# Out-projection of a two-layer encoder: early products placed by hand in the last head, and the first MLP weight splits queued behind the last pair's split

## The chip, the cores and the metric

The kernel runs on one core of one Trainium2 chip. The core has a matrix engine (TensorE, PE in the profile; its weight loads are the row PEld), a vector engine (VectorE, DVE), an activation engine (ScalarE, ACT), a general engine (GpSimd, POOL) and a queue that issues DMAs (SyncE, SP). Each engine executes its own queue in order and waits on semaphores for the others. The metric is the device time of one execution in microseconds (us); less is better.

## The reference, cut to what matters

Two layers over a sequence of 512 tokens with 1024 features, in float32. Each layer does, with shifts, scales and gates from a conditioning vector:

```
h  = rms_norm(x, g) * (1 + sc1) + sh1
q_d, k_d, v_d, cq, ckv, k_rope = split(h @ w_in)
o_dil = dilated_attention(q_d, k_d, v_d)        # 8 heads of 64
o_mla = latent_attention(cq, ckv, k_rope)       # 8 heads of 64
x  = x + gt1 * (concat[o_dil, o_mla] @ w_out)   # the out-projection
h  = rms_norm(x, g) * (1 + sc2) + sh2
x  = x + gt2 * (square(relu(h @ W1)) @ W2)      # the MLP, 4096 wide
```

The change is about the line of the out-projection and what stands next to it: the last heads of the latent attention before it, the norm and the MLP behind it.

## The kernel before

**Precision by splitting.** Every large float32 operand x is split into hi = round(x) in the PE's faster format and lo = x - hi. A product is then three matmuls into the same PSUM bank: hi by hi, lo by hi and hi by lo (`mm3`, L237 to L240). `load_split` (L229) loads a weight tile into a `raw` buffer by DMA (L232), makes hi on ACT (L233) and lo on POOL (L234).

**Layout.** x is held transposed, as eight tiles of 128 features by 512 tokens (`xT`, j = 0 to 7). A product with the token axis cut in two (`HALF`) is 256 columns wide.

**Attention.** Eight pairs of heads run one after the other (stages st = 0 to 7; pairs 0 to 3 dilated, 4 to 7 latent). `head` (L327) does, for each of four query blocks qb: scores into a PSUM bank `sc` (two buffers), the row maximum on DVE (L346), the exponential on ACT (L347), a reciprocal (L348), the scaling on ACT, DVE or POOL (L351 to L355), four transposes on PE into a bank `tr` (L358, two buffers), and the split of the transposed block (hi on ACT, L361; lo on DVE, L362) into `pt` buffers. Behind the four blocks come sixteen value products (L368), and the two halves of their result are added into the pair's `o` (ACT L370, DVE L371). Once both heads of a pair are done, `o` is split into `ot`: hi on ACT (L651), lo on POOL (L652). These splits, `OT[0]` to `OT[7]`, are what the out-projection multiplies: its input features are 8 groups of 128, one for each pair.

**Out-projection.** `out_dil(j)` multiplies the four dilated pairs, full width, in the stages of the latent heads, and adds into x (`add_x`, L659). `out_lat(j, p, hf, ks, ...)` multiplies the latent pairs ks for one half of the tokens: for k = 0, 1, 2 that needs only the first three latent pairs, for k = 3 the last pair. For the first half the program does k = 0 to 2 for all eight j behind the heads: j = 4 to 7 are added into x at once, j = 0 to 3 are held in the four `mm` banks; then k = 3 for all j. Then `norm` of the first half, all of the second half (8 x 12 matmuls), `norm` of the second half, and the MLP, whose first product takes the first half. The norm squares x tile by tile on ACT (L255, L258), sums on DVE (L259), sums over partitions with a matmul by ones (L284), and makes h in eight chunks.

**The MLP's weights.** `w1_tile(i)` is a `load_split` into the `pt` buffers (i = 0, 1; the last head's own buffers before), the `qk` buffers (i = 2, 3) or the `wh`, `wl` buffers.

**What sets the order.** The program is traced as Python runs it. `heads` is a generator that yields after each query block and after the values, ten times for a pair; `weave` calls the events of the stage whose due time (in yields, table TUNE) is past. The traced order is only a priority: a planner walks through the program with its own model of each instruction's time, and puts on every engine's queue, at each moment, the earliest traced instruction that it takes to be ready and whose buffers are free. So instructions that are ready early move ahead of earlier traced ones that wait. `tc.keep_in_program_order(ins)` ties one instruction behind the one traced just before it on the same engine; it ties nothing else. On the chip the queues are then served strictly in the planned order.

## Time and profile before

| | |
|---|---|
| runs | 1353.67 us median of 3 (1353.58 to 1356.93) |
| profiled execution | 1351.23 us, of which the trace spans 1349.5 us |
| mean granted clock of PE | 0.973 |
| PE busy | 1271.8 us |
| DMA | 167.62 MB, 124 GB/s on average |

A row of the timeline gives start, duration, engine, line of the program, operation and tiles (out<-in), and in brackets how long the engine was idle before it and who ended that. A row of the table by windows gives, for a stretch of the span, its length, and for each engine the busy time and the number of instructions; PEclk is the clock that PE was granted, 1.00 being full speed. Matmuls overlap in PE, so that the distance between two starts and not the duration of one says what a matmul costs in a row of them. The heads of the last pair (stage 7) run from 311.59 to 336.32 us in layer 0 and from 951.00 to 973.41 in layer 1, counted from the start of L370 for the head before to the first product of the last pair.

### The profile page before, as it was taken

To read this page: it belongs to the slowest core of one execution; us is meant where nothing else is said; L and a number is where in the kernel's file an instruction comes from. 1 tells how busy PE (TensorE), PEld (TensorE's weight loads), DVE (VectorE), ACT (ScalarE), POOL (GpSimd) and SP (SyncE) were. 2 spreads that over 40 slices of the span, in tenths; PEclk is the share of its full clock that TensorE was granted. 3 is DMA by queue.
4 is the path that set the end of the run, shared out by engine and by line. 5 is a ranking of instruction groups with operands and counts; after the bars stand their busy time and mean duration, and the time that the engine had idled before them with its cause. 6 is when DMAs were issued, how large, how long until landed. Compare 5 with 4: busy or idle time off the path is not lost.

```text
span 1349.5 us, 19637 instructions
## 1 busy us (share of the span) xinstructions
PE 1271.8 (94%) x7114; PEld 1116.2 (83%) x7114; DVE 761.6 (56%) x1644; ACT 680.4 (50%) x1421; POOL 653.0 (48%) x504
## 2 busy tenths in 40 slices
PE   4889989898999999999999999899799999999999
PEld 2778867777998888888899999798699888888888
DVE  6777787875763561834576678987573122121123
ACT  5567898776542332322247677887653232232321
POOL 5636786674445444444438333545443444444441
PEclk6979989999999999999999999999999999999999
DMA  9335543341244572754534243211111322233221
GB/s 343 113 102 173 182 155 103 105 134 62 71 164 165 185 266 94 266 172 157 167 122 129 79 136 123 85 48 63 60 51 54 103 94 94 94 99 104 94 94 63
DMA packets 57248, 167.62 MB, mean 124 GB/s; under 512 B 8640, under 2 KB 10816, under 8 KB 57152
## 3 DMA queue, kind: packets, MB, share of 16 engines
q1 hardware_dynamic: 57152, 166.38, 37.5%
q8 instruction: 56, 0.92, 0.3%
q14 instruction: 40, 0.33, 0.1%
HBM read 155.87 MB, written 10.49 MB: 123 GB/s over the span
## 4 chain that ended last, share of the span: by engine, by line
PE 66%; POOL 2%; DVE 2%; ACT 2%; issue 2%; DMA 1%; POOLq 0%; DVEq 0%; ACTq 0%
PE mm L240 20%; PE mm L238 20%; PE mm L239 20%; PE tr L368 2%; PE tr L358 1%; POOL wl L234 1%; PE sc L238 1%; PE sc L239 1%; PE sc L240 1%; POOL pt L234 1%; PE sc L482 0%; PE mm L469 0%; DVE pt L362 0%; PE sc L483 0%; PE mm L626 0%
## 5 line engine op out<-in xcount | busy, mean ns | idle before, releaser
L234 POOL TENSOR_TENSOR wl<-raw,wh 128x1024 fp32r<-128x1024 f32 (+3 forms) x174 | 395.7, 2276 | 440.1 <-ACT wh L233 436.4
L233 ACT ACTIVATE wh<-raw 128x1024 fp32r<-128x1024 f32 (+3 forms) x174 | 174.6, 1004 | 263.9 <-PE mm L240 211.7
L659 DVE SCALAR_TENSOR_TENSOR x<-mm,mod,x 128x512 f32<-128x512 f32 (+1 forms) x152 | 92.4, 620 | 255.7 <-PE mm L240 255.2
L238 PE MATMUL mm<-h,wh 128*128 128x512 f32 (+1 forms) x544 | 198.5, 365 | 0.2
L239 PE MATMUL mm<-h,wl 128*128 128x512 f32 (+1 forms) x544 | 198.1, 364 | 0.0
L240 PE MATMUL mm<-h,wh 128*128 128x512 f32 (+1 forms) x544 | 197.9, 364 | 0.0
L238 PE MATMUL mm<-ot,wh 128*128 128x512 f32 (+1 forms) x416 | 147.9, 357 | 7.3 <-ACT ot L651 5.2
L843 ACT ACTIVATE P<-mm 128x512 f32<-128x512 f32 (+1 forms) x80 | 41.1, 513 | 214.3 <-PE mm L240 208.2
L239 PE MATMUL mm<-ot,wl 128*128 128x512 f32 (+1 forms) x416 | 146.7, 354 | 0.0
L240 PE MATMUL mm<-ot,wh 128*128 128x512 f32 (+1 forms) x416 | 144.2, 354 | 2.2 <-POOL ot L652 2.2
L844 DVE SCALAR_TENSOR_TENSOR mm<-mm,P 128x512 f32<-128x512 f32 (+1 forms) x80 | 46.9, 589 | 132.1 <-ACT P L843 132.1
L238 PEld LDWEIGHTS mm<-h,wh 128*128 128x128 f32 x544 | 102.6, 189 | 16.8 <-DVE qk L846 0.6
L239 PEld LDWEIGHTS mm<-h,wl 128*128 128x128 f32 x544 | 102.7, 189 | 16.1
L240 PEld LDWEIGHTS mm<-h,wh 128*128 128x128 f32 x544 | 102.6, 189 | 16.2
L238 PE MATMUL mm<-qk,wh 128*128 128x512 f32 (+1 forms) x288 | 105.3, 366 | 1.0 <-DVE x L659 1.0
L239 PE MATMUL mm<-qk,wl 128*128 128x512 f32 (+1 forms) x288 | 105.3, 365 | 0.0
L240 PE MATMUL mm<-qk,wh 128*128 128x512 f32 (+1 forms) x288 | 105.2, 365 | 0.0
L170 DVE SCALAR_TENSOR_TENSOR pt<-pt,cb 128x1024 f32<-128x1024 f32 x56 | 100.6, 1828 | 0.0
L355 POOL TENSOR_SCALAR P<-P,hs 128x512 f32<-128x512 f32 x64 | 48.4, 756 | 106.0 <-DVE hs L348 85.2
L362 DVE TENSOR_TENSOR pt<-tr,pt 128x512 fp32r<-128x512 f32 x128 | 86.6, 683 | 19.1 <-ACT pt L361 18.5
L238 PEld LDWEIGHTS mm<-ot,wh 128*128 128x128 f32 x416 | 80.1, 193 | 19.2 <-ACT ot L651 5.7
L238 PE MATMUL mm<-wh,h 128*128 128x384 f32 x240 | 81.0, 352 | 11.8 <-ACT h L742 9.8
(290 smaller groups left out, 2980.2 us busy)
## 6 DMA issues: line engine op xcount, KB each, us to landing
raw<-in_w_dram SPq DMA_DIRECT2D x64, 512.0 KB, 3.4
pt<-in_wmod_dram SPq DMA_DIRECT2D x56, 512.0 KB, 4.8
raw<-in_w2a_dram SPq DMA_DIRECT2D x48, 512.0 KB, 3.5
raw<-in_wmod_dram SPq DMA_DIRECT2D x24, 512.0 KB, 3.6
raw<-in_win_dram SPq DMA_DIRECT2D x30, 384.0 KB, 3.1
bias<-b SPq DMA_DIRECT2D x32, 256.0 KB, 2.3
raw<-in_wout_dram SPq DMA_DIRECT2D x16, 512.0 KB, 3.7
raw<-in_w2b_dram SPq DMA_DIRECT2D x16, 512.0 KB, 3.4
```

The costliest lines, as they stand in the source:

```text
L170: r = V.scalar_tensor_tensor(w, w, 1.0, cb, op0=OP.mult, op1=OP.mult, accum_out=out)
L233: A.activation(hi, raw, AF.Copy)
L234: G.tensor_tensor(lo, raw, f(hi), op=OP.subtract)
L238: T.matmul(out, sh, mh, start=first, stop=False)
L239: T.matmul(out, sl, mh, start=False, stop=False)
L240: T.matmul(out, sh, ml, start=False, stop=last)
L355: G.tensor_scalar(P, P, r_, 0.0, op0=OP.mult, op1=OP.add)
L362: V.tensor_tensor(lo, tr, f(hi), op=OP.subtract)
L368: T.matmul(po[:, HALF[qh]], vals(hd, kc), pt[qh][w][:, kc], start=(kc == 0 and w == 0), stop=(kc == 3 and w == 1))
L659: V.scalar_tensor_tensor(xT[j][:, hf], p, gt[:, j:j + 1], xT[j][:, hf], op0=OP.mult, op1=OP.add)
L843: A.activation(r, p, AF.Relu)
L844: V.scalar_tensor_tensor(p, p, 0.0, r, op0=OP.max, op1=OP.mult)
```

## The change

It has two parts. The first concerns the out-projection's products for the first half of the tokens with k = 0, 1, 2. They are now traced inside the last pair's heads, by a function `early(j)`: j = 0, 1, 2 as events with due times 5.5, 6.5 and 7.5 of stage 7, that is in the second head of the pair behind query blocks 0, 1 and 2; j = 3 behind the last block's scores, j = 4 behind its transposes, j = 5 and 6 behind the values (by calls of a `hook` in `head`); j = 7 behind the heads. The first matmul of each but j = 7 is tied to the PE instruction traced just before it. j = 0 to 3 are now added at once and j = 4 to 7 held, the other way round than before, and k = 3 begins with the held ones. The out-projection's weights of the latent half are due earlier (0.5 to 5 instead of 3.5 to 10.04).

The second part traces the MLP's weight tiles 0 to 3 right behind the heads instead of at the MLP, and ties the ACT half and the POOL half of tile 0 to the instructions traced just before them on ACT and POOL, which are the last pair's split (L651 and L652).

```diff
-    OL0=(3.5, 3.5), OL1=(10.04, 10.04), MV0=(1.5,), MV1=(3.75,), MV2=(5.37,), MV3=(8,), MV4=(0.62,),
+    OL0=(0.5, 0.5), OL1=(5, 5), OE=(5.5, 5.5), MV0=(1.5,), MV1=(3.75,), MV2=(5.37,), MV3=(8,), MV4=(0.62,),
...
-    def load_split(src, n, raw="raw", tags=("wh", "wl")):
+    def load_split(src, n, raw="raw", tags=("wh", "wl"), keep=False):
         SY.dma_start(raw, src)
-        A.activation(hi, raw, AF.Copy)
-        G.tensor_tensor(lo, raw, f(hi), op=OP.subtract)
+        ra = A.activation(hi, raw, AF.Copy)
+        rg = G.tensor_tensor(lo, raw, f(hi), op=OP.subtract)
+        if keep:
+            tc.keep_in_program_order(ra)
+            tc.keep_in_program_order(rg)
...
-    def mm3(out, sh, sl, mh, ml, first, last):
-        T.matmul(out, sh, mh, start=first, stop=False)
+    def mm3(out, sh, sl, mh, ml, first, last, pin=False):
+        r = T.matmul(out, sh, mh, start=first, stop=False)
+        if pin:
+            tc.keep_in_program_order(r)
...
+            if qb == 3:
+                hook("score")
...
+            if qb == 3:
+                hook("turned")
...
+        hook("values")
...
+                hook = (lambda at: [early(j) for j in EARLY[at]]) if st == 7 and hd else (lambda at: None)
+                yield from head(l, 2 * pr + hd, hd, w["score"], bias, w["vals"], o, hook)
...
+        EARLY = dict(score=(3,), turned=(4,), values=(5, 6))
+        held = {}
+
+        def early(j, pin=True):
+            p = ps("mm")[:, :256]
+            out_lat(j, p, HALF[0], (0, 1, 2), True, j < 4, pin)
+            if j < 4:
+                add_x(j, HALF[0], p, gt1)
+            else:
+                held[j] = p
...
+                ev += [(tn("OE") + j, lambda j=j: early(j)) for j in range(3)]
...
+        ws1 = [w1_tile(i, i == 0) for i in range(4)]
+        hf = HALF[0]
+        early(7, False)
         for j in (4, 5, 6, 7, 0, 1, 2, 3):
-            p = ps("mm")[:, :256]
-            out_lat(j, p, hf, (0, 1, 2), True, j >= 4)
-            if j >= 4:
-                add_x(j, hf, p, gt1)
-            else:
-                held[j] = p
-        for j in range(8):
-            p = held[j] if j < 4 else ps("mm")[:, :256]
-            out_lat(j, p, hf, (3,), j >= 4, True)
+            p = held[j] if j >= 4 else ps("mm")[:, :256]
+            out_lat(j, p, hf, (3,), j < 4, True)
             add_x(j, hf, p, gt1)
...
-            ws = [w1_tile(i) for i in range(8)] if grp[0] == 0 else []
+            ws = ws1 + [w1_tile(i) for i in range(4, 8)] if grp[0] == 0 else []
```

More of the change, by code (lines that the diff above doesn't have):

```diff
@@ L325, in distances, with head @@
         return dist, g
-    def head(l, h, hd, score, bias, vals, o):
+    def head(l, h, hd, score, bias, vals, o, hook=lambda at: None):
         pt = [(t4("pt", [128, 4, 256]), t4("pt", [128, 4, 256])) for _ in range(2)]
@@ L648, in heads @@
             for hd in range(2):
-                yield from head(l, 2 * pr + hd, hd, w["score"], bias, w["vals"], o)
+                hook = (lambda at: [early(j) for j in EARLY[at]]) if st == 7 and hd else (lambda at: None)
+                yield from head(l, 2 * pr + hd, hd, w["score"], bias, w["vals"], o, hook)
             ot = t4("h" if st in (2, 3) else "ot", [128, 2, S])
@@ L665, in out_load, with out_lat @@
             wo[half, jj] = (hi.rearrange("p (j k m) -> p j k m", j=2, k=4), lo.rearrange("p (j k m) -> p j k m", j=2, k=4))
+        EARLY = dict(score=(3,), turned=(4,), values=(5, 6))
+        held = {}
+        def out_lat(j, p, hf, ks, first, last, pin=False):
+            wh, wl = wo[1, j // 2]
+            for k in ks:
+                mm3(p, wh[:, j % 2, k], wl[:, j % 2, k], OT[4 + k][:, 0, hf], OT[4 + k][:, 1, hf],
+                    first and k == ks[0], last and k == ks[-1], pin and k == ks[0])
+        def early(j, pin=True):
[5 more added lines that the diff above has]
+                held[j] = p
         def out_dil(j):
@@ L805, in trunk, with w1_tile @@
         h2h, h2l = new_h()
[L807 to L825 removed]
+        def w1_tile(i, pin=False):
+            tags = ("wh", "wl") if i >= 4 else ("pt", "pt") if i < 2 else ("qk", "qk")
+            return tuple(t.rearrange("p (k m) -> p k m", k=8) for t in load_split(a["w1"][l, i], 1024, tags=tags, keep=pin))
+        ws1 = [w1_tile(i, i == 0) for i in range(4)]
+        hf = HALF[0]
+        early(7, False)
+        for j in (4, 5, 6, 7, 0, 1, 2, 3):
+            p = held[j] if j >= 4 else ps("mm")[:, :256]
+            out_lat(j, p, hf, (3,), j < 4, True)
             add_x(j, hf, p, gt1)
@@ L846, in mlp1_post @@
             V.tensor_tensor(r2[:, 1, hf], p, f(r2[:, 0, hf]), op=OP.subtract)
-        def w1_tile(i):
-            tags = ("wh", "wl") if i >= 4 else ("pt", "pt") if i < 2 else ("qk", "qk")
-            return tuple(t.rearrange("p (k m) -> p k m", k=8) for t in load_split(a["w1"][l, i], 1024, tags=tags))
         R2 = {}
```

6 lines of the change are left out of this document (removed).

## The prediction

> **What bounds the kernel now.** I read the page first, then the busy time of each engine by stage, then the timelines of PE, POOL and ACT around the end of attention in both layers.
>
> ```profile
> span 1349.5 us, 19637 instructions
> ...
> PE 1271.8 (94%) x7114; PEld 1116.2 (83%) x7114; DVE 761.6 (56%) x1644; ACT 680.4 (50%) x1421; POOL 653.0 (48%) x504
> ```
>
> PE is busy for 94% of the span, so only two things can pay: time in which PE is idle, and time in which its clock is low. Both must be looked for in the stage that the change touches. I cut layer 1 at the starts of L370, which each head executes once behind its last value product; the last two borders are the first product of the last pair and the first MLP product.
>
> ```profile
> core 0: us, PE busy (x) PEld busy (x) DVE busy (x) ACT busy (x) POOL busy (x), PEclk, DMA share, GB/s
> ...
> 934.05:942.72 8.67, 8.67 (x62) 7.67 (x61) 6.14 (x13) 7.29 (x17) 4.90 (x4) 1.00 0.18 60
> 942.72:951.00 8.28, 7.33 (x46) 5.63 (x44) 6.15 (x13) 6.80 (x16) 1.33 (x3) 1.00 0.01 2
> 951.00:963.69 12.69, 11.43 (x84) 10.27 (x83) 7.79 (x17) 8.35 (x17) 5.31 (x5) 1.00 0.04 13
> 963.69:973.41 9.72, 5.52 (x43) 4.66 (x40) 4.21 (x7) 8.28 (x13) 4.55 (x2) 1.00 0.25 94
> 973.41:992.74 19.33, 17.50 (x123) 16.92 (x124) 11.80 (x30) 9.08 (x19) 10.06 (x6) 0.82 0.30 93
> ```
>
> Rows one and two are the next-to-last pair's heads, three and four the last pair's, five the rest of the out-projection. The last head keeps PE busy for only 5.52 of 9.72 us, and in the last row the clock is 0.82. Layer 0 has the same shape:
>
> ```profile
> 291.00:303.05 12.05, 9.22 (x54) 7.97 (x53) 9.23 (x16) 9.48 (x19) 10.81 (x7) 0.86 0.61 186
> 303.05:311.59 8.54, 8.09 (x59) 7.19 (x57) 6.14 (x12) 7.16 (x14) 3.30 (x3) 1.00 0.29 98
> 311.59:324.52 12.93, 12.24 (x87) 10.92 (x86) 8.38 (x19) 9.14 (x19) 4.37 (x5) 1.00 0.02 8
> 324.52:336.32 11.80, 6.55 (x40) 5.01 (x38) 4.21 (x7) 7.83 (x12) 7.90 (x5) 0.81 0.29 94
> 336.32:354.37 18.05, 17.66 (x123) 17.08 (x123) 11.79 (x30) 9.20 (x19) 8.74 (x5) 0.84 0.31 101
> ```
>
> The waits themselves, from PE's timeline (in brackets the idle time and who ended it), layer 1 and then layer 0:
>
> ```profile
> 967.94 0.63 PE L358 MATMUL tr<-ident,P 128*128 128x128 f32 x4 [1.53 <-DVE pt L362]
> 968.94 2.18 PE L368 MATMUL tr<-pt,qk 128*128 128x256 f32 x16 [0.38 <-DVE pt L362]
> 973.41 0.44 PE L238 MATMUL mm<-ot,wh 128*128 128x256 f32 x1 [2.29 <-ACT ot L651]
> ...
> 974.72 0.41 PE L238 MATMUL mm<-ot,wh 128*128 128x256 f32 x1
> 974.93 0.41 PE L239 MATMUL mm<-ot,wl 128*128 128x256 f32 x1
> 977.18 1.22 PE L240 MATMUL mm<-ot,wh 128*128 128x256 f32 x4 [1.83 <-POOL ot L652]
> ...
> 980.21 0.38 PE L240 MATMUL mm<-ot,zz 128*128 128x256 f32 x1
> ```
>
> ```profile
> 328.05 0.63 PE L358 MATMUL tr<-ident,P 128*128 128x128 f32 x4 [0.80 <-DVE pt L362]
> ...
> 330.96 0.38 PE L368 MATMUL tr<-pt,qk 128*128 128x256 f32 x1 [1.09 <-ACT pt L361]
> 331.69 1.71 PE L368 MATMUL tr<-pt,qk 128*128 128x256 f32 x7 [0.34 <-DVE pt L362]
> 336.32 0.58 PE L238 MATMUL mm<-ot,wh 128*128 128x256 f32 x1 [2.93 <-ACT ot L651]
> ...
> 338.79 1.22 PE L240 MATMUL mm<-ot,wh 128*128 128x256 f32 x4 [0.39 <-POOL ot L652]
> ```
>
> In the last head 1.53 + 0.38 + 2.29 = 4.20 us are idle in layer 1, and 0.80 + 1.09 + 0.34 + 2.93 = 5.16 in layer 0; behind it 1.83 and 0.39 us go to the lo half of the last pair. From 973.41 to 980.21 a 256-column matmul starts every 0.21 us (974.72, 974.93). At full clock they follow at 12.00 / 101 = 0.12:
>
> ```profile
> 981.00:993.00 12.00, 12.00 (x101) 11.95 (x100) 8.86 (x23) 7.30 (x14) 6.60 (x3) 1.00 0.23 73
> ```
>
> Some 22 matmuls run at the slow pitch (8 hi products, 4 lo, about 10 more), which loses 22 x 0.09 = 2.0 us in each layer.
>
> Nothing to fill these waits with is left, because the planner has spent it. The products of the first three pairs (k 0 to 2 of the first half of the columns, 8 x 9 = 72 matmuls) need nothing of the last head and ran earlier. A third of them are L239; layer 1's first and second head of the last pair, then layer 0's:
>
> ```profile
> L239 PE MATMUL mm<-ot,wl 128*128 128x256 f32 x10 | 2.8, 282 | 0.0
> ...
> L239 PE MATMUL mm<-ot,zz 128*128 128x256 f32 x2 | 0.5, 282 | 0.0
> ...
> L239 PE MATMUL mm<-ot,wl 128*128 128x256 f32 x4 | 1.2, 302 | 0.0
> ```
>
> ```profile
> L239 PE MATMUL mm<-ot,wl 128*128 128x256 f32 x11 | 3.1, 282 | 0.0
> ...
> L239 PE MATMUL mm<-ot,zz 128*128 128x256 f32 x2 | 0.5, 283 | 0.0
> ...
> L239 PE MATMUL mm<-ot,wl 128*128 128x256 f32 x3 | 0.9, 308 | 0.0
> ```
>
> So about 36 fall into the first head of the pair and 12 into the second in layer 1 (39 and 9 in layer 0), the remaining 24 earlier. In the first head they filled no wait: 36 x 0.12 = 4.3 us, and that head takes 12.69 - 8.28 = 4.4 us more than the product-free head before it. They are plain added time there and would be free in the last head.
>
> **The change, part by part.** The first edit traces the products inside the last head and ties the first matmul of j = 0 to 6 behind the PE instruction traced just before it. For j = 1, 2 that is the transposes of query blocks 1 and 2, for 3 the last score, for 4 the last transposes, for 5 and 6 the values; j = 7 is not tied but traced last. For j = 0 it is only the long-finished product of the dilated half, so j = 0 stays free to run in the first head. Per layer:
>
> *Earlier heads.* 24 products leave. In layer 1, 15 of them stood in the head of 8.67 us, which may fall to 8.28 (0.4 us), and 9 before it, worth 0 to 1.1; I take 0.9 together (0.4 to 1.5). In layer 0 the stage of 12.05 us, with its clock of 0.86, could fall at most to the next head's 8.54; but its ACT also waits for weights, so I take 0.8 (0 to 3.5).
>
> *First head of the last pair.* 36 products leave (4.3 us; layer 0: 39, 4.7). j = 0 comes in at 0 to 1.1 us; I take 0.5. Saved: 3.8 (3.2 to 4.3) and 4.2 (3.6 to 4.7).
>
> *Last head.* It now holds 63 products instead of 12 (9): 51 x 0.12 = 6.1 us more (54: 6.5). The idle 4.20 (5.16) is filled first. The order is fixed and the queue serves it strictly, so products ahead of a transpose can delay the chain, and the adds of j = 1 to 3 (L659) enter DVE between the chain's steps; both show as waits left over. No row shows their size: below zero they can't be, since the waits are already counted as gone, and the longest wait of the stage, 2.29 (2.93), is the other end. I take 1.0, nearer to the end where products are at hand. The head grows by 6.1 - 4.2 + 1.0 = 2.9 us (1.9 to 4.2), in layer 0 by 6.5 - 5.2 + 1.0 = 2.3 (1.3 to 4.3).
>
> *Behind the last head.* The second edit traces the first four MLP weight tiles right behind the heads and ties tile 0's ACT and POOL halves behind the last pair's. Now they stand in front:
>
> ```profile
> 971.78 1.06 ACT L233 ACTIVATE pt<-raw 128x1024 fp32r<-128x1024 f32 x1
> 972.75 0.61 ACT L651 ACTIVATE ot<-o 128x512 fp32r<-128x512 f32 x1
> ...
> 983.88 1.06 ACT L233 ACTIVATE wh<-raw 128x1024 fp32r<-128x1024 f32 x1 [0.54 <-PE mm L240]
> ```
>
> ```profile
> 971.22 4.69 POOL L234 TENSOR_TENSOR pt<-raw,pt 128x1024 fp32r<-128x1024 f32 x2 [2.20 <-ACT pt L233]
> 975.84 1.28 POOL L652 TENSOR_TENSOR ot<-o,ot 128x512 fp32r<-128x512 f32 x1
> ```
>
> POOL does two splits (4.69 us) and only then the lo half, 2.5 us after its hi was there (972.75 + 0.61). With both behind, lo is done about 1.3 us after hi, and product 7 (9 x 0.12 = 1.1 us) and the eight hi products (1.0) cover that: the 1.83 (0.39) goes. If tile 1, which is not tied, still goes first, half of the 4.69 stays and up to 1.6 us of wait in layer 1 (0.4 in layer 0). The splits now end some 5 us later than before; the MLP needs them at 992.74, so that is hidden, and their two raw buffers come free later for the next loads, whose next split stood at 983.88 and waited for PE. The loads of the out-projection's weights, whose due times the change brings forward too, are all issued long before the last pair:
>
> ```profile
> 863.39 41.49 SPq L232 DMA_DIRECT2D raw<-in_wout_dram  x4
> ```
>
> The planner is ahead of the program here, so on SP nothing is moved past that anyone waits for. With PE busy without a break I take the half-clock loss of 2.0 us as gone too.
>
> What is late next is the norm. It starts from the adds of the first half and must be ready when PE has done the second half's 96 products:
>
> ```profile
> 983.72 0.41 DVE L259 TENSOR_TENSOR P<-sc,s 128x256 f32<-128x256 f32 x1
> ...
> 986.54 0.42 DVE L285 TENSOR_SCALAR P<-tr 128x256 f32<-128x256 f32 x1 [0.73 <-PE tr L284]
> ```
>
> The sum of squares is there at 984.13, but DVE gets its product only at 986.54, so some 1.3 us of this chain are queueing on PE and shorten with it, while a faster PE takes about 1.3 us off the cover (14 matmuls behind 977.18 x 0.09). I take 0.5 us as lost (0 to 1.3). Saved behind the last head: 1.8 + 2.0 - 0.5 = 3.3 (at best 3.8, at worst 3.8 - 1.3 - 1.6 = 0.9), in layer 0: 0.4 + 2.0 - 0.5 = 1.9 (2.4, and 2.4 - 1.3 - 0.4 = 0.7).
>
> **Sum.** Layer 1: 0.9 + 3.8 - 2.9 + 3.3 = 5.1. Layer 0: 0.8 + 4.2 - 2.3 + 1.9 = 4.6. Together 9.7 us. The profiled execution took 1351.23 us (span 1349.5), and would take 1341.5; against the median of the runs, 1353.67, the forecast is 1344.0. All favourable ends give 7.7 + 9.3 = 17.0 (1336.7), all unfavourable ones 0.3 + 0.0, which is no change (1353.4).
>
> **The clock, weighed.** The clock still stood at 1.00 in the stage up to 973.41 and fell to half behind idle times of 1.53, 0.38 and 2.29 us. The Trainium skill, "TensorE: Matmul & The Clock Gate", section "Why this matters for your kernels", asks only that no idle gap be longer than about 3 us. By that rule the 2.0 us per layer would not have been lost, and the sum without them would be 5.7. The trace decides: the loss is there, after shorter gaps.
>
> **The rivals.** (1) *The change does only part of what it says.* Tile 1 is not tied and goes ahead of the last pair's lo half, and the norm comes late: the last stage then saves 0.9 and 0.7 instead of 3.3 and 1.9, and the time is 1344.0 + 3.6 = 1347.6. For it: a single tie; against it: PE reaches the lo products later than now. Chance 0.10.
>
> (2) *The tail moves instead of going.* The products stand ahead of the chain's transposes, run out before the last hi half is there, and the waits of 2.29 and 2.93 us come back: the unfavourable ends, 1353.4. For it: the order is fixed by hand, and DVE and ACT have their own work between the steps (ACT 8.28 of 9.72 us busy in the last head). Chance 0.14.
>
> (3) *Slower: the clock falls in the heads that lose their products.* Two heads per layer then run on scores, transposes and values alone. The head that does so now is PE-busy for 7.33 of 8.28 us; at the slow pitch (0.21 for 0.12) this becomes 12.8 us, 4.5 more. Two heads in each of two layers: 18.0, and 1344.0 + 18.0 = 1362.0. It decides from the point where more than about half of those heads' time runs at half clock, which eats the 9.7. For it: the clock fell behind a stretch with transposes and waits. Against it: that product-free head ran at 1.00. The same page, section "Part 4: PE-mode transpose", says that transposes don't count as busy for the clock; no run here separates that. Chance 0.10.
>
> **How the numbers follow.** The forecast's own case has 0.66. Times within 0.3% (4.1 us, about what a measurement of this kernel can tell from no change) lie between 1349.6 and 1357.7. Faster: 0.66 + 0.10 = 0.76; the same: 0.14; slower: 0.10. The range leaves out the extreme favourable corner and rival 3, and reaches to rival 2: 1338.5 to 1353.0.
>
> **What would show it.** Right: the first head of the last pair near 8.8 us instead of 12.69; the last head longer than now, with PE busy for 90% of it or more; no clock below 1.00 behind it; L652 directly behind L651 and before the splits of tiles 0 and 1; the first MLP product right behind the last out-projection product. Wrong: a wait of 2 us or more before the last pair's first product, a clock of 0.5 in either head, or PE waiting for the norm by more than 1.3 us.

## The result, and the profile after

The changed kernel took 1346.21 us (median of 4 runs, 1343.71 to 1348.03) against 1353.62 (1353.1 to 1356.93) for the kernel before on the same chip: ratio 0.9943, interval 0.9929 to 0.9956. In a second set of runs, beside experiments 8 to 10, it took 1344.41 (6 runs, 1342.63 to 1349.75) against 1353.41: 0.9937 (0.9921 to 0.9954). The profiled execution is the 1343.71 of the first four.

The page's first lines:

```profile
span 1341.6 us, 19641 instructions
...
PE 1263.8 (94%) x7114; PEld 1108.2 (83%) x7114; DVE 762.4 (57%) x1644; ACT 679.8 (51%) x1421; POOL 652.0 (49%) x504
```

The span is 7.9 us shorter and PE's busy time 8.0, with the same 7114 matmuls. The busy time of each engine by stage, cut at the same five places as before (the "L370" of the cut is now L380), layer 0 and then layer 1:

```profile
core 0: us, PE busy (x) PEld busy (x) DVE busy (x) ACT busy (x) POOL busy (x), PEclk, DMA share, GB/s
291.55:302.17 10.62, 7.67 (x47) 5.87 (x46) 9.05 (x15) 8.77 (x16) 10.41 (x6) 1.00 0.62 195
302.17:311.25 9.08, 7.82 (x50) 6.07 (x48) 6.20 (x13) 8.47 (x19) 3.76 (x3) 1.00 0.32 100
311.25:319.63 8.38, 7.01 (x46) 5.82 (x45) 6.78 (x14) 7.67 (x16) 2.63 (x3) 1.00 0.06 24
319.63:332.89 13.26, 12.02 (x97) 11.34 (x96) 6.05 (x12) 7.55 (x14) 7.13 (x5) 1.00 0.24 80
332.89:350.42 17.53, 15.37 (x124) 14.90 (x123) 12.04 (x30) 9.03 (x18) 12.21 (x6) 1.00 0.38 125
```

```profile
928.87:937.53 8.66, 7.71 (x50) 6.12 (x49) 6.14 (x13) 7.28 (x16) 4.88 (x4) 1.00 0.18 61
937.53:945.82 8.29, 7.34 (x46) 5.64 (x44) 6.14 (x13) 6.80 (x15) 1.33 (x3) 1.00 0.01 2
945.82:955.78 9.96, 7.84 (x50) 6.14 (x49) 6.60 (x14) 8.27 (x18) 4.35 (x4) 1.00 0.00 0
955.78:967.97 12.19, 11.16 (x95) 10.93 (x93) 5.48 (x10) 7.50 (x13) 4.30 (x4) 1.00 0.27 89
967.97:985.51 17.54, 15.37 (x125) 14.91 (x123) 12.05 (x30) 9.04 (x18) 12.22 (x6) 1.00 0.39 123
```

The third row of each is the first head of the last pair without its products, the fourth the last head with them: PE is busy there for 91% and 92% of the time (55% and 57% before), and no row has a clock below 1.00. In layer 0 the five stages lose 1.43, gain 0.54, lose 4.55, gain 1.46 and lose 0.52 us: -4.48 in sum (before minus after row by row, with 291.00 as the first border before). In layer 1: -0.01, +0.01, -2.73, +2.47, -1.79: -2.05. What is left of the 7.9 lies outside these stages: -1.23 from layer 0's MLP to 928.87, -0.67 behind 985.51, and +0.55 ahead of 291.55.

POOL's timeline around the last pair's split in layer 1 shows the second part of the change at work:

```profile
966.98 1.29 POOL L663 TENSOR_TENSOR ot<-o,ot 128x512 fp32r<-128x512 f32 x1 [3.82 <-ACT ot L662]
968.24 4.76 POOL L234 TENSOR_TENSOR pt<-raw,pt 128x1024 fp32r<-128x1024 f32 x2
```

The lo half (L663) is made first, 0.71 us behind the start of its hi half (966.27), and the two weight splits behind it. Both waits that PE had for the last pair are gone. The last head still has some idle time, at another place than before: 1.03 us in layer 1 and 1.24 in layer 0, ahead of its own transposes (PE's groups of transposes in the last head, layer 1 and then layer 0; behind the second bar the idle time in front of them and who ended it):

```profile
L365 PE MATMUL tr<-ident,P 128*128 128x128 f32 x16 | 2.4, 276 | 1.0 <-DVE o L381 1.0
...
L365 PE MATMUL tr<-ident,P 128*128 128x128 f32 x15 | 2.4, 280 | 1.2 <-POOL P L362 0.9 <-DVE o L381 0.4
```

And one longer wait is new, in both layers (PE's timeline):

```profile
350.42 0.39 PE L241 MATMUL mm<-h,pt 128*128 128x256 f32 x1 [1.94 <-ACT h L279]
...
985.51 0.39 PE L241 MATMUL mm<-h,pt 128*128 128x256 f32 x1 [1.94 <-ACT h L279]
```

PE has finished the out-projection and waits 1.94 us for the norm's first h. The kernel before did not wait there (its MLP began at 354.37 and 992.74 without idle time in front). The norm's chain is L264 (DVE, the last row of the sum of squares), L289 (PE, product with ones), L290 (DVE), L291 and L292 (ACT, logarithm and exponential), L293 to L295 and L278 (DVE), L279 (ACT, the first h). L670 is the residual add of an output into x. DVE's timeline in layer 1, then two rows of ACT's and one of PE's:

```profile
976.91 0.42 DVE L264 TENSOR_TENSOR P<-sc,s 128x256 f32<-128x256 f32 x1
...
980.45 0.42 DVE L290 TENSOR_SCALAR P<-tr 128x256 f32<-128x256 f32 x1 [1.09 <-PE tr L289]
...
982.17 0.49 DVE L670 SCALAR_TENSOR_TENSOR x<-mm,mod,x 128x256 f32<-128x256 f32 x1 [0.90 <-PE mm L245]
982.57 0.41 DVE L293 TENSOR_TENSOR P<-P,tr 128x256 f32<-128x256 f32 x1
983.01 0.42 DVE L294 SCALAR_TENSOR_TENSOR P<-P,tr 128x256 f32<-128x256 f32 x1
983.60 0.48 DVE L670 SCALAR_TENSOR_TENSOR x<-mm,mod,x 128x256 f32<-128x256 f32 x1 [0.17 <-PE mm L245]
984.00 0.42 DVE L295 SCALAR_TENSOR_TENSOR tr<-P,tr 128x256 f32<-128x256 f32 x1
984.46 0.49 DVE L278 SCALAR_TENSOR_TENSOR sc<-x,al,tr 128x256 f32<-128x256 f32 x1
```

```profile
980.73 1.06 ACT L233 ACTIVATE wh<-raw 128x1024 fp32r<-128x1024 f32 x1 [1.94 <-PE mm L245]
981.69 0.40 ACT L291 ACTIVATE P<-P 128x256 f32<-128x256 f32 x1
```

```profile
979.74 0.59 PE L289 MATMUL tr<-P,ones 128*128 128x256 f32 x2
```

The sum of squares is there at 977.33 (976.91 + 0.42), and the product with ones starts on PE at 979.74, 2.41 us later, behind products of the second half. (Before, it started 1.71 us behind the sum: 985.84 after 984.13.) On ACT the chain's logarithm, whose input is there at 980.87, stands behind a weight split that waited 1.94 us for PE to free its buffer. And on DVE the residual add of 983.60 stands between L294 and L295: it is the second half's last one, and waits for PE's last product. From there each step follows the one before it without idle time: 983.60 add, 984.00 L295, 984.46 L278, 984.98 L279, 985.51 PE. So the chain can be late for three reasons: its place on PE, the split on ACT and the add on DVE. The experiments weigh them.

### The profile page after: what moved, and what is told of

Same layout as the page of the kernel before. It is cut to its first block, busy times and chain, and to the rows that moved or that the text cites. A ratio compares the mean times of both kernels' runs of the same rounds, so it can differ in the third digit from the quotient of the medians.

```text
span 1341.6 us, 19641 instructions
## 1 busy us (share of the span) xinstructions
PE 1263.8 (94%) x7114; PEld 1108.2 (83%) x7114; DVE 762.4 (57%) x1644; ACT 679.8 (51%) x1421; POOL 652.0 (49%) x504
## 4 chain that ended last, share of the span: by engine, by line
PE 75%; DVE 6%; ACT 5%; DMA 3%; POOL 3%; issue 2%; DVEq 0%; ACTq 0%; POOLq 0%
PE mm L241 22%; PE mm L244 22%; PE mm L245 22%; PE tr L377 3%; PE tr L365 2%; DMA raw<-in_wout_dram 1%; DVE pt L371 1%; POOL wl L234 1%; DVE P L350 1%; ACT P L354 1%; PE sc L241 1%; ACT wh L233 1%; POOL raw L167 1%; PE sc L244 1%; PE sc L492 1%
## 5 line engine op out<-in xcount | busy, mean ns | idle before, releaser
L670 DVE SCALAR_TENSOR_TENSOR x<-mm,mod,x 128x512 f32<-128x512 f32 (+1 forms) x152 | 92.4, 621 | 255.1 <-PE mm L245 254.5
L362 POOL TENSOR_SCALAR P<-P,hs 128x512 f32<-128x512 f32 x64 | 48.1, 751 | 99.9 <-DVE hs L355 81.0
L365 PE MATMUL tr<-ident,P 128*128 128x128 f32 x512 | 77.5, 275 | 15.7 <-DVE o L381 6.1
```

Source lines behind the costliest of these rows:

```text
L362: G.tensor_scalar(P, P, r_, 0.0, op0=OP.mult, op1=OP.add)
L365: T.transpose(tr[:, kc], P[:, kc * 128:(kc + 1) * 128], ident)
L670: V.scalar_tensor_tensor(xT[j][:, hf], p, gt[:, j:j + 1], xT[j][:, hf], op0=OP.mult, op1=OP.add)
```

## The experiments

Experiments 1, 2 and 4 take the change apart. 3, 5 and 8 look for the cause of the new wait, 6 for the length of the last pair's first head, 7 and 10 for what the clock answers to; 9 joins 6 and 8.

A stage of one profiled execution repeats within 0.1 us from execution to execution (the last pair's first head and what follows, in the changed kernel's second profile: 8.44, 30.81, 9.95 and 29.72 us against 8.38, 30.79, 9.96 and 29.73), while whole times spread by some 5 us in one kernel; where layer 0's second head of the next-to-last pair begins varies from 300.94 to 306.56 us alone. So the verdicts below rest on stages and waits first and on medians second. "Last stage" is the stretch from the last head's start to the MLP's first product: 29.85 us (layer 0) and 29.05 (layer 1) before, 30.79 and 29.73 after.

**1. The products alone.** The changed kernel without its second part:

```diff
-        ws1 = [w1_tile(i, i == 0) for i in range(4)]
...
-            ws = ws1 + [w1_tile(i) for i in range(4, 8)] if grp[0] == 0 else []
+            ws = [w1_tile(i) for i in range(8)] if grp[0] == 0 else []
```

> The changed kernel without its second part: the products are placed by hand, but the MLP's tiles 0 to 3 are traced at the MLP and tied to nothing. My theory: tiles 0 and 1 are free as soon as the last values are done and go ahead of the last pair's lo half on POOL again (4.7 us); PE, which now reaches the lo products about 4 us after the values, waits for them 2 to 3 us in each layer, so most of the gain is lost: 1349 to 1352 us, with a PE wait on the last pair's POOL split of 2 us or more in both layers. Rival: the products cover that wait by themselves, and the second part is worth only the 1.83 and 0.39 us it had before: 1346 to 1348 us.

1350.75 us (1349.35 to 1354.07), ratio 0.9977 (0.9968 to 0.9986), as the theory has it. PE's timeline, layer 0 and then layer 1:

```profile
340.29 0.50 PE L245 MATMUL mm<-ot,wh 128*128 128x256 f32 x2 [1.92 <-POOL ot L663]
...
976.30 0.50 PE L245 MATMUL mm<-ot,wh 128*128 128x256 f32 x2 [1.93 <-POOL ot L663]
...
994.40 0.39 PE L241 MATMUL mm<-h,pt 128*128 128x256 f32 x1 [1.94 <-ACT h L279]
```

The earlier kernel's waits in the last head are gone (1.03 and 1.24 us at its transposes are left, as in the changed kernel), and the one for POOL's lo half is there at full size: the two parts answer for different waits. And the two layers differ in two points: the same wait of 1.92 us left the clock at 1.00 in layer 0 and took it down in layer 1,

```profile
340.29:345.67 5.38, 5.15 (x39) 4.95 (x40) 4.55 (x12) 2.12 (x6) 0.00 (x0) 1.00 0.21 84
```

```profile
976.30:981.68 5.38, 5.16 (x28) 4.95 (x28) 4.09 (x10) 2.03 (x5) 0.00 (x0) 0.68 0.21 81
```

11 matmuls fewer in the same 5.38 us. And the norm's wait of 1.94 us is there in layer 1 and not in layer 0. Both come back below.

**2. The splits alone**: the kernel before with the second part of the change, first with the old due times of the out-projection's weights, then with the change's.

```diff
+        ws1 = [w1_tile(i, i == 0) for i in range(4)]
...
-            ws = [w1_tile(i) for i in range(8)] if grp[0] == 0 else []
+            ws = ws1 + [w1_tile(i) for i in range(4, 8)] if grp[0] == 0 else []
```

```diff
-    OL0=(3.5, 3.5), OL1=(10.04, 10.04),
+    OL0=(0.5, 0.5), OL1=(5, 5),
```

> The kernel before with the second part of the change alone: tiles 0 to 3 traced right behind the heads, tile 0 tied behind the last pair's split. My theory: the wait on POOL (1.83 and 0.39 us) goes, but the waits in the last head and the half clock stay, and the norm takes part of it back: 1351.5 to 1353 us. Rival: this part carries half of the gain or more: 1350 us or less.

1352.64 us (1350.83 to 1355.3), 0.9992 (0.9983 to 1.0001): no change that can be measured. The waits for POOL stayed (2.53 us in layer 1, 0.90 in layer 0), with both weight splits still ahead of the lo half. A tie holds on to the instruction traced just before it, and with the old due time 10.04 that is the split of the out-projection's last weights, traced behind the heads and done long ago. So this run did not test the splits; it showed that the new due times are part of the change, for a reason that the prediction had not seen. With them:

> The kernel before with the change's second part: the first four weight tiles asked for in front of the closing products, the first one's split tied, and the out-projection's weight loads at the change's earlier due times, without which the tie held on to a weight split long done. The products stay as before. Theory: POOL's order now has the last pair's low part ahead of the two splits, so the wait for it falls from 1.83 us in layer 1 and 0.39 us in layer 0 to under 0.2 us; the waits in the last head (1.53, 0.38 and 2.29 us in layer 1) and the lowered clock behind it stay. The stretch from the last head's start to the MLP's first product falls from 29.05 to 27 to 27.8 us in layer 1 and by 0 to 0.8 us in layer 0: time 1351 to 1352.5. Rival: the clock behind the last head was held down by the wait for POOL as much as by the waits in the head; then it goes back to 0.95 or more and layer 1's stretch falls below 26.5 us, time 1349.5 to 1351.

1348.46 us (1344.24 to 1352.73), 0.9969 (0.9956 to 0.9981). The waits for POOL were 0.16 us and none; the last stage of the profiled execution was 28.10 and 27.84 us. The theory's stage for layer 1 came out just above its range (27 to 27.8), layer 0 fell by 1.75 where 0 to 0.8 was expected (with POOL's wait, 0.9 us of the one for the hi half went: 2.06 for 2.93), and the median lies beyond both theories' times; the profiled execution, 1352.0, is near the upper end of its own runs. In it PE's waits were 1.52, 0.38 and 2.06 us in layer 1's last head, and the clock already fell behind the first two:

```profile
970.80 3.67 PE L371 MATMUL tr<-pt,qk 128*128 128x256 f32 x16 [0.38 <-DVE pt L365]
```

These sixteen value products took 2.18 us before. The two parts alone take off 3.0 and 4.6 us, together the change takes 7.4 and, in the second set of runs, 9.0: within the spread of the runs they add up.

**3. The order of the adds.** j = 4 to 7 added early and 0 to 3 held, as it was before:

```diff
-        EARLY = dict(score=(3,), turned=(4,), values=(5, 6))
+        EARLY = dict(score=(7,), turned=(0,), values=(1, 2))
...
-            out_lat(j, p, HALF[0], (0, 1, 2), True, j < 4, pin)
+            out_lat(j, p, HALF[0], (0, 1, 2), True, j >= 4, pin)
...
```

> The changed kernel with the roles of the column tiles swapped: j = 4 to 7 are added early and j = 0 to 3 held, so that the last products and adds begin with j = 0, as in the kernel before. The changed kernel has a new PE wait of 1.94 us for the norm in each layer. My theory: it comes from the order of the adds, because the sum of squares begins with x[0], whose last add now comes fifth; with the swap the sum is ready 1.0 to 1.5 us earlier, the wait falls to 0.5 to 1 us, and the time is 1.5 to 3 us less than the changed kernel's 1346.2: 1343 to 1345. Rival: the wait is there only because PE gets to the MLP earlier, and the norm's chain is set by its places in the queues of PE and ACT: the wait stays within 0.4 us and the time at 1346 +- 1.

1345.78 us (1342.64 to 1348.83), 0.9936 (0.9924 to 0.9949), the wait for the norm 1.94 us in both layers. The theory that the swapped order of the adds makes the norm late has fallen; its rival, the places in the queues, is left.

**4. The products without the ties**, traced at the same places:

```diff
-                    first and k == ks[0], last and k == ks[-1], pin and k == ks[0])
+                    first and k == ks[0], last and k == ks[-1], False)
```

> The changed kernel with the products traced at the same places but none of their matmuls tied. My theory: tracing is only a priority, so the planner runs them as early as they are ready, in the heads before, the waits in the last head come back (4 us or more idle in layer 1) and with them the half clock: 1350.5 to 1353 us. Rival: the traced place is enough, because earlier traced work is preferred whenever it is ready: 1345 to 1347.5 us.

1351.28 us (1349.31 to 1354.63), 0.9986 (0.9975 to 0.9997). The planner runs the products early again: the last pair's first head is 13.10 and 12.70 us, and the waits in the last head are back (1.56, 0.38 and 2.06 in layer 1; 2.00, 0.20 and 2.06 in layer 0), with a granted clock of 0.94 from the last head's start to the MLP in both. Where a line is traced is only a priority here; the tie does the work.

**5. Tile 7's split out of the chain's way** on ACT: tiles 4 to 6 traced ahead of the first half's norm, tile 7 behind it and tied.

```diff
+        ws1 += [w1_tile(i) for i in range(4, 7)]
         norm(hf, amlp[l], modc[l][:, 24:32], h2h, h2l)
+        ws1.append(w1_tile(7, True))
```

> The changed kernel, but the first group's weight tiles 4 to 6 are asked for ahead of the first half's norm and tile 7 behind it, its split held behind the norm's last chunks on ACT and POOL. Theory: the 1.94 us that PE waits for the norm in both layers is the norm's chain standing in its engines' queues behind entries that wait for PE. Of these tile 7's split on ACT is one: it waits 1.94 us for PE to free its buffer, and the logarithm, whose input is ready at 980.87, runs only at 981.69 behind it; with the logarithm ahead of the split, DVE's later steps also stand one residual add earlier each. So PE's wait falls from 1.94 to between 0.7 and 1.2 us in both layers, nothing else moves, and the time is 1.5 to 2.5 us under the changed kernel's 1346.2: about 1344.2. Rival: DVE's residual adds, which wait for PE too, set the chain alone; then the wait stays at 1.8 to 1.95 us and the time at 1346.

1346.53 us (1345.5 to 1348.37), 0.996 (0.9948 to 0.9972). PE's timeline in layer 1:

```profile
986.29 0.38 PE L241 MATMUL mm<-h,pt 128*128 128x256 f32 x1 [1.48 <-ACT h L279]
...
999.52 0.38 PE L241 MATMUL mm<-h,wh 128*128 128x256 f32 x1 [1.03 <-DVE qk L870]
```

The wait falls to 1.48 in both layers, half as much as was expected, and in both layers a new wait (the 1.03 of the second row; 363.84 in layer 0) gives more than that back; the time is the rival's. ACT has its logarithm right behind L290 now (982.16, where L290 started at 981.70), so the split was no longer in the way, but DVE's timeline shows what ends the chain:

```profile
984.26 0.43 DVE L295 SCALAR_TENSOR_TENSOR tr<-P,tr 128x256 f32<-128x256 f32 x1
984.85 0.48 DVE L670 SCALAR_TENSOR_TENSOR x<-mm,mod,x 128x256 f32<-128x256 f32 x1 [0.16 <-PE mm L245]
985.25 0.48 DVE L278 SCALAR_TENSOR_TENSOR sc<-x,al,tr 128x256 f32<-128x256 f32 x1
```

The last add, which waits for PE's last product, now stands one step further down, behind L295: the wait is shorter by that one step (984.00 to 984.46 in the changed kernel, 0.46) and by nothing else. In this order it is the add that ties the end of the chain to PE's end.

**6. All four early splits tied**, to take tile 3's out of the last pair's first head:

```diff
-        ws1 = [w1_tile(i, i == 0) for i in range(4)]
+        ws1 = [w1_tile(i, True) for i in range(4)]
```

> The changed kernel, but the first four weight splits are all tied behind the last pair's split, where the change ties only the first. Theory: the last pair's first head is 9.96 us in layer 1 where 8.8 was forecast because tile 3's split stands in it, 1.06 us on ACT ahead of an exponential and 2.40 us on POOL ahead of a row scaling for which the head waits. With tiles 2 and 3 behind the last head, that head falls to 8.7 to 9.2 us in layer 1 and stays within 0.4 of 8.38 in layer 0; the splits then fill ACT and POOL behind the last head, where the wait for the norm stays at 1.94 or grows to at most 2.6 us. Time 1344.5 to 1346. Rival: the head's length is its own chain of exponential, scaling, transposes and copies with little to cover it, and the split only fills gaps: 9.8 to 10 us as before, time 1346 to 1347.5.

1345.55 us (1343.95 to 1346.87), 0.9951 (0.9939 to 0.9963). Layer 1's first head, and the first 10 us of its MLP:

```profile
946.36:955.24 8.88, 7.73 (x50) 6.14 (x49) 6.51 (x14) 7.21 (x17) 2.65 (x4) 1.00 0.00 0
```

```profile
985.00:995.00 10.00, 10.00 (x71) 10.00 (x72) 6.45 (x17) 5.48 (x13) 6.96 (x9) 0.83 0.32 107
```

9.96 became 8.88: tile 3's split cost that head 1.08 us, as the theory says. In layer 0, where of this split only the ACT half had stood in the first head (312.51), that head grew by 0.48, a little more than expected, but the stages around it shrank (8.06, 8.86 and 29.90 for 9.08, 8.38 and 30.79): 1.43 less in sum. Of these 2.5 us the time shows little (1345.55; the changed kernel 1346.21 and 1344.41). In the profiled execution they were given back behind the stages: from layer 0's MLP to layer 1's heads it took 1.87 us longer than the changed kernel, and from layer 1's MLP to the end 1.5. The second row shows one reason: the wait for the norm, 1.98 us here, was followed by a lowered clock (in layer 0 too). The changed kernel's own row is

```profile
985.51:995.51 10.00, 10.00 (x82) 9.95 (x83) 7.54 (x20) 6.96 (x17) 5.12 (x8) 1.00 0.13 48
```

**7. Work in POOL's wait.** The kernel of experiment 1 with 14 products of no use in front of the closing ones:

```diff
+        dummy = ps("sc")[:, :256]
+        for i in range(14):
+            r = T.matmul(dummy, wo[1, 2][0][:, 0, 0], OT[4][:, 0, hf], start=i == 0, stop=i == 13)
+            tc.keep_in_program_order(r)
```

> The kernel with the products' part alone, and in its wait of 1.92 us for POOL 14 further products of 128 x 256 into a bank that nobody reads (work that the reference does not have), tied behind the products that precede the wait. They are 14 x 0.12 = 1.7 us at full clock. In layer 1 that kernel ran its next products at a pitch of 0.21 instead of 0.12 us from 976.6 to about 981, a granted clock of 0.95 over the stage, and the stage is 33.34 us against the changed kernel's 29.73, of which the wait explains 1.93. Theory: the lowered clock follows PE's idle time; with PE busy in it the clock stays at 1.00, and the stage falls by 1.2 to 1.8 us, to 31.5 to 32.1, while the low part arrives no earlier; layer 0, whose clock was 1.00, stays within 0.4 of 30.86. Time about 1349.5. Rival: the clock falls for another reason (the density of the products in front of it, or chance from one execution to another): layer 1 stays at 0.95 and 33.3, or layer 0 falls as well.

1349.85 us (1346.61 to 1352.27), 0.9981 (0.9969 to 0.9992). The last stages, layer 0 and then layer 1:

```profile
319.61:352.62 33.01, 29.33 (x234) 27.99 (x232) 18.07 (x42) 16.70 (x31) 19.34 (x10) 1.00 0.29 99
```

```profile
958.84:990.80 31.96, 28.48 (x232) 27.57 (x229) 17.52 (x40) 16.64 (x30) 16.52 (x9) 1.00 0.30 101
```

Layer 1 went from 33.34 to 31.96 us with the clock at 1.00: the low clock had cost 1.38 us beside the wait. One pair of executions can't tell by itself that it was the answer to the wait, since the same wait left layer 0's clock at 1.00 in experiment 1; the section on the hardware gives the reason. Layer 0 went the other way, from 30.86 to 33.01, and this was not expected: the norm's wait of 1.94 us, which experiment 1 did not have there, appeared. In experiment 1's queues two residual adds stood behind L295 in layer 0 and none in layer 1; here it is none in both.

**8. The chain ahead of the last adds.** Four of the second half's eight outputs are traced ahead of the norm, and the fifth's first product is tied behind the product with ones. That product then has 48 of the second half's 96 products behind it in PE's queue (27 in the changed kernel, 54 and 56 before), and the planner puts L295 and L278 ahead of the last two adds.

```diff
+        def half1(j, pin):
+            p = ps("mm")[:, :256]
+            out_lat(j, p, HALF[1], (0, 1, 2, 3), True, True, pin)
+            add_x(j, HALF[1], p, gt1)
+
+        for j in range(4):
+            half1(j, False)
         norm(hf, amlp[l], modc[l][:, 24:32], h2h, h2l)
         hf = HALF[1]
-        for j in range(8):
-            p = ps("mm")[:, :256]
-            out_lat(j, p, hf, (0, 1, 2, 3), True, True)
-            add_x(j, hf, p, gt1)
+        for j in range(4, 8):
+            half1(j, j == 4)
```

> The changed kernel, but four of the eight second-half outputs are traced ahead of the first half's norm and the first product of the fifth is tied behind the norm's product with ones. That product then stands in PE's queue behind 48 of the second half's 96 products, where it stood behind 68: 20 x 0.12 = 2.4 us earlier, at about 977.4 in the changed kernel's layer 1, when the sum of squares (ready at 977.33) is just there. On ACT the logarithm and the exponential now stand ahead of tile 7's split. Theory: PE's 1.94 us in front of the MLP is the norm's chain held back by the places of its steps in the queues, PE's first of all, and not the chain's own length; the wait goes to 0 to 0.4 us in both layers, the stretch from the last head's start to the MLP falls by 1.5 to 1.9 us in each, and the time is 2.5 to 4 us under the changed kernel's. Rival: the chain from squares to h is itself the length of what is left, so that an earlier product with ones only makes PE wait for the sum of squares instead, with the same total: the wait moves and the time stays within 1 us.

1343.23 us (1341.1 to 1344.57), 0.9919 (0.9907 to 0.9931), the fastest kernel of this study. The last stages:

```profile
323.14:352.25 29.11, 27.55 (x219) 26.41 (x218) 17.98 (x42) 17.41 (x33) 18.49 (x10) 1.00 0.31 109
```

```profile
958.07:986.03 27.96, 26.61 (x218) 25.95 (x215) 17.42 (x40) 17.36 (x32) 15.68 (x9) 1.00 0.33 113
```

The wait is gone in both layers and the last stages are 1.68 and 1.77 us shorter, as the theory has it. Behind them 1.1 us are given back (against the changed kernel's second profile 0.5 from MLP to heads, 0.6 to the end), so that 2.4 of 3.5 us are left in the profile. DVE's timeline in layer 1 has the adds behind the chain,

```profile
983.75 0.42 DVE L295 SCALAR_TENSOR_TENSOR tr<-P,tr 128x256 f32<-128x256 f32 x1
...
985.66 0.48 DVE L670 SCALAR_TENSOR_TENSOR x<-mm,mod,x 128x256 f32<-128x256 f32 x1
```

although a weight split still waits for PE on ACT ahead of the first h. Against the changed kernel in the same runs (1344.41) the median is 1.2 us lower where 2.5 to 4 were expected, and the two intervals overlap, so the stages carry this verdict and not the medians. The edit moves two things at once, the product with ones on PE and the adds on DVE; what each is worth is weighed below.

**9. The edits of 6 and 8 together.**

> The earlier product with ones together with all four splits tied behind the last pair's split, the version that should be best. If the two are separate terms, the last pair's first head in layer 1 is 8.9 us (9.96 in the changed kernel), layer 0's last three heads and what follows are 1.4 us shorter together, and the wait for the norm is under 0.6 us in both layers: 1.0 + 1.4 + 2 x 1.6 = 5.6 us under the changed kernel in the stages, a time 3.5 to 5.5 us under it. Rival: the four splits, now all behind the last head, stand in the norm's way on ACT (two of the later tiles' splits stand between its logarithm and the first h), the wait comes back at 1 to 2 us and the time is that of the earlier product alone or more.

1345.78 us (1343.64 to 1348.46), 0.9942 (0.9928 to 0.9956): the gain in the stages is there (layer 0's last three heads and what follows 45.23 us for 48.25, layer 1's last two 37.02 for 39.69, together 5.7) and is given back behind them. PE's timeline, layer 0 and 1, and POOL's in layer 1:

```profile
354.13 0.39 PE L245 MATMUL mm<-h,pt 128*128 128x256 f32 x1 [2.51 <-POOL h L276]
...
989.11 0.39 PE L245 MATMUL mm<-h,pt 128*128 128x256 f32 x1 [2.17 <-POOL h L276]
```

```profile
977.68 9.61 POOL L234 TENSOR_TENSOR wl<-raw,wh 128x1024 fp32r<-128x1024 f32 x4
987.29 1.08 POOL L275 TENSOR_SCALAR b<-b,al,mod 128x256 f32<-128x256 f32 x2
```

With eight weight splits behind the last head POOL is busy with them until 987.29, and the norm's chunks that POOL makes come behind. The rival named ACT; it is POOL.

**10. Work in the last head's waits**, in the kernel with the splits alone: 10 useless products behind its last scores and 14 behind its values.

```diff
+        def warm(n):
+            d = ps("sc")[:, :256]
+            for i in range(n):
+                r = T.matmul(d, wo[1, 0][0][:, 0, 0], OT[4][:, 0, HALF[0]], start=i == 0, stop=i == n - 1)
+                tc.keep_in_program_order(r)
...
```

> The splits' part alone, with products of no use (10 behind the last head's last scores, 14 behind its values; 128 x 256 into a bank that nobody reads, work that the reference does not have) tied into PE's two longest waits of the last head. The kernel without them showed 1.52, 0.38 and 2.06 us of waiting in layer 1, then the clock at half (its 16 value products took 3.67 us where 2.18 is usual; 0.88 over the stage), and its executions spread from 1344.2 to 1352.7. Theory: the half clock is the answer to PE's idle time and is a cost beside the waits; 10 x 0.12 = 1.2 and 14 x 0.12 = 1.7 us of work inside the waits delay nothing that is on the path, keep the clock at 1.00, and take 1.5 to 3 us off the stage of each layer (27.84 and 28.10): 1345 to 1347, with a spread of under 5 us. Rival: the idle time does not set the clock, or the added work delays the head: stages of 27.8 us or longer, 1348.5 or more.

1348.42 us (1345.78 to 1354.71), 0.9967 (0.9955 to 0.9979): as without them. Layer 1's last head and what follows, and PE's wait:

```profile
963.41:973.50 10.09, 8.43 (x67) 7.61 (x64) 4.12 (x7) 6.36 (x12) 2.36 (x1) 1.00 0.25 90
973.50:991.55 18.05, 15.72 (x122) 15.06 (x123) 12.07 (x30) 10.05 (x19) 13.19 (x6) 1.00 0.36 121
```

```profile
991.55 0.39 PE L241 MATMUL mm<-h,pt 128*128 128x256 f32 x1 [1.94 <-ACT h L277]
```

Half of the theory held: with PE busy the clock stayed at 1.00, and 28.14 less 1.94 of waiting is 26.20 against 27.84, so the low clock had cost about 1.64 us. But all of it was given back: the planner's new order has no add behind L295 (two without the useless products), and the norm's wait took the place of the low clock.

**11. The changed kernel again**, on the chip and in the hour of 8 to 10:

> The changed kernel once more, on the chip and in the hour of the three kernels below, so that they stand beside it. The medians so far differ by up to 0.7 us from batch to batch, and the stretches ahead of the change alone start up to 4 us apart from execution to execution, so 1345 to 1347.5, and the stages of the last pair within 0.15 us of its first profile: 8.38, 30.79, 9.96 and 29.73 us.

1344.41 us, just under what was expected, with the stages as expected.

**The wait for the norm, over all kernels**, by the number of the second half's adds that the order of DVE's queue has behind L295 (L290 in the kernel before; the same step under other numbers in 2 and 10):

| adds behind L295 | kernels and layers | PE's wait, us |
|---|---|---|
| 2 | before, 2 (both due times) and 8, both layers; 1, layer 0 | none |
| 1, ahead of L278 | 5, both layers | 1.48 |
| 0 | changed kernel, 3, 4, 6, 7 and 10, both layers; 1, layer 1 | 1.94 to 1.98 |

There is no exception. (9 has two, one of them ahead of L278, and no wait in front of the MLP, but the two on POOL behind its start.) With none behind, the wait has a fixed length: add, L295, L278 and L279 follow PE's last product. In experiment 4's layer 1 the product with ones stood 6.36 us ahead of the MLP where it stood 5.76 to 5.81 ahead in the 14 others, and the wait was 1.95 all the same.

The table has a second reading, though, and no run separates the two by itself. With no add behind L295 the product with ones had 27 products behind it on PE (32 in experiment 4's layer 1), with two it had 43 to 56: a chain that starts late finds the adds ahead of it. An estimate from the rows above tells how much is whose. In experiment 5, with the logarithm free, L293 started 1.33 us behind L290 (981.70, 983.03), and L294 and L295 can follow by 0.44 us each. From 980.45 the changed kernel's L295 could so have started at 982.66, where it started at 984.00. Of the 1.94 us some 1.3 are thus entries that wait for PE and stand ahead of the chain's steps, the adds on DVE and the weight split on ACT, and some 0.6 the late place of the product with ones on PE.

## Why the prediction was right, and where it was not

The forecast was 1344.0 us and "faster"; the medians are 1346.21 and 1344.41. The mechanism was the forecast's own case: products moved from where they were plain time to where PE waited, POOL's order turned round, the clock at 1.00. The sum was 9.7 us and the traced span shows 7.9, of which 6.5 lie in the stages of the forecast. The other 1.4 come from stretches for which it had no term, and the medians of the two sets of runs differ by 1.8, so that how near they come to 1344.0 is in part luck. Saved, in us, layer 1 and layer 0:

| step | forecast | measured |
|---|---|---|
| earlier heads | 0.9 / 0.8 | 0.0 / 0.9 |
| first head of the last pair | 3.8 / 4.2 | 2.73 / 4.55 |
| last head grows by | 2.9 / 2.3 | 2.47 / 1.46 |
| behind the last head | 3.3 / 1.9 | 1.79 / 0.52 |

*Behind the last head* holds the term that was mis-sized most: "I take 0.5 us as lost (0 to 1.3)" for the norm. It is 1.94 in each layer, beyond the bound, and by the forecast's own sign ("PE waiting for the norm by more than 1.3 us") this step was wrong. With 1.94 in its place the step's other terms come out: 1.83 + 2.0 - 1.94 = 1.9 (1.79 measured) and 0.39 + 2.0 - 1.94 = 0.45 (0.52). The forecast took the chain's queueing on PE to get shorter and the cover to shrink by about 1.3 us. The queueing got longer instead: in layer 1 the product with ones comes 2.41 us behind the sum of squares where it was 1.71. And the cover shrank by half, to 27 products behind the product with ones, where it was 54 and 56. On DVE, where the forecast had not looked, the last add, which waits for PE's last product, now stands ahead of L295, so that in this order no cover on PE can help. What the clock gave, the norm took: experiment 10 shows this exchange by itself. (In experiment 7's layer 0 the norm's wait came without any gain of the clock.) The 2.0 for the clock itself was near: 1.38 and 1.64 us where it was isolated.

*First head, layer 1*: 1.1 us short, as much as tile 3's split cost there (1.08, experiment 6), which the second part of the change let into that head and which the forecast had only looked for behind the last head. *Last head*: the leftover waits were sized well, 1.03 and 1.24 us for 1.0, though for another reason than it gave: by the profile the head's transposes wait for the last add of the head before (L381) and, in layer 0, for POOL's scaling (L362). The head grew by less than forecast since PE's busy time grew by 5.6 and 5.5 us for 6.1 and 6.5; in layer 0 the clock of this head also rose from 0.81 to 1.00, which the forecast had not counted. *Earlier heads, layer 1*: the head of 8.67 us lost 12 products and no time, so they had filled its waits (PE's busy time there fell from 8.67 to 7.71). The rivals: the last pair's lo half does go first and the waits of 2.29 and 2.93 us did not come back, so (1) and (2) are out, except that (1) had named a late norm; (3) is out, with a clock of 1.00 in every head that lost its products. Of the forecast's signs of being right two did not come: layer 1's first head is 9.96 us long and not near 8.8, and the MLP's first product does not follow the last out-projection product directly.

## What to carry to other kernels

When work is moved in a kernel whose queues a planner lays out, look on every engine of the next chain for an entry that waits for the engine which has just been filled: one such entry ahead of a late step ties the chain to that engine's end, and the gain goes there. Count too how much work the planner has left behind that chain's first step on the filled engine. A tie binds an instruction to what is traced just before it, so a due time elsewhere can decide what it means. Judge such changes by stages of the trace, which repeat within 0.1 us where whole times spread by several.

## What the hardware showed

A wait of PE of about 1.94 us sometimes costs a second time. In the 10 us behind the norm's wait of 1.94 to 1.98 us PE ran either 82 to 83 matmul rows with a clock of 1.00 or 69 to 71 with 0.83, and nothing between; 12 x 0.12 = 1.4 us. Over the profiled executions here it fell behind 7 of 15 such waits: in none of the changed kernel's four and of experiment 4's two, in both layers of experiments 6 and 7, in one layer of 3 and 10, and in experiment 1's one. A clock of 0.83 over 10 us is 10 x 0.17 / 0.5 = 3.4 us at half, and so is experiment 1's 0.68 over 5.38. Experiment 9's waits of 2.51 and 2.17 us had it behind the shorter one only; behind experiment 5's two of 1.48 us it stayed at 1.00.

The traces tell what decides. In each of the 14 profiled executions the clock changes only at the points of a grid of 3.413 us. In the changed kernel's, for example, half-clock stretches begin at 53.36, 73.84, 80.67 and 90.91 us, which lie 6, 2 and 3 times 3.413 apart. Where the grid stands against the program differs from execution to execution. For the norm's 15 waits, the share of a grid interval in which PE was idle (the largest that the wait made):

| the wait | waits | idle share of the interval | clock in the next interval |
|---|---|---|---|
| whole in one interval | 7 | 0.57 to 0.58 | half |
| cut by a point of the grid | 8 | 0.31 to 0.54 | full |

So the same wait goes both ways by where the grid cuts it. Experiment 1's two layers fit: POOL's wait made 0.52 of an interval idle in layer 1, with half clock behind it, and 0.43 and 0.20 of two in layer 0; with useless work in it (experiment 7) no interval there was idle for more than 0.11. Over all intervals at full clock behind the first 34 us of the 14 executions, half clock followed 65 of 66 that were idle for 0.55 or more, none that was idle for less than 0.30, and some of those between. The exact measure is not shown.

The length agrees with what the Trainium skill, "TensorE: Matmul & The Clock Gate", section "Part 1: The HAM clock gate", says of an activity window of about 3.4 us that runs freely. The forecast had weighed the rule of gaps under about 3 us on the same page of the Trainium skill, section "Why this matters for your kernels"; here waits of 1.93 and 1.94 us took the clock down.

The changed kernel keeps two such waits and experiment 8's none: its runs spread by 3.5 us where the changed kernel's spread by 4.3 and 7.1, which fits, in few runs.

What stays open: where experiment 6's gain went beyond its one profile, and why the stretch ahead of the change varies by up to 5.6 us between executions. In one pair the difference is PE's own pace: up to the second head of the next-to-last pair the same 1424 matmul rows took 247.43 us of PE time in the changed kernel's second profile (41.0 us at half clock) and 252.35 in experiment 8's (51.2 us), with that head beginning at 300.94 and 305.68.
